# The first feed-forward's input products as seven half-size products for eight, with the gated values in DRAM

## The chip, the cores and the metric

The kernel runs on one core of one Trainium2 chip. The metric is the device time of one execution in microseconds (us); before is the kernel without the change, after the kernel with it. TensorE is called PE here, VectorE DVE, ScalarE ACT, GpSimd POOL and SyncE SP, as the profile names them; PEld is PE's loading of weights.

## The reference, cut to what matters

The whole is a two-layer model with 512 latent and 256 context tokens, and a second block of two layers behind it. The change lies in the feed-forward of the first layer, which runs over all 768 tokens. Its matrices are 1024 x 5632 (`ffn_w_in`, gate and value side by side) and 2816 x 1024 (`ffn_w_out`):

```
def swiglu(h, w_in, w_out):
    a, b = jnp.split(h @ w_in, 2, axis=-1)
    return (jax.nn.silu(a) * b) @ w_out
...
        x = x + g1 * rmsnorm(y_lat, norm_g[l, 1])
        f_lat = swiglu(rmsnorm(x, norm_g[l, 2]) * (1.0 + sc2) + sh2, ffn_w_in[l], ffn_w_out[l])
        x = x + g2 * rmsnorm(f_lat, norm_g[l, 3])
...
            ctx_s = ctx_s + cg1 * rmsnorm(y_ctx, norm_g[l, 1])
            f_ctx = swiglu(rmsnorm(ctx_s, norm_g[l, 2]) * (1.0 + csc2) + csh2, ffn_w_in[l], ffn_w_out[l])
```

`sc2`, `sh2`, `g2` and the like are parts of `silu(c) @ ada_w[l] + ada_b[l]`, for the latent vector `c` and for the context vector. All of it is float32.

## The kernel before

A float32 product is made of three products of a shorter format: each operand is split into a high part `h` (a copy by ACT that rounds) and a low part `l` (a subtraction by DVE), and `mm3` adds `wh*xh`, `wh*xl` and `wl*xh` in PSUM (L329, L330, L331). The splits are `split` for data (ACT L321, DVE L322) and `load_w` for weights (ACT L312, DVE L314). `load_w` loads blocks of 128 x 1024 (512 KB) into `wr`, which has three buffers, by SP's queue (L310); `wh` and `wl` have four each. An instruction waits in its engine's queue, and all that stands behind it there waits too; the order in each queue is set by a scheduler when the kernel is built.

The stretch around the change has three stages.

**Mixer's output.** `layer0_mixer` ends with `out_phase` over `w0_out`. Its last three weight blocks are used tile by tile (six tiles of 128 tokens, 18 matmuls each, `acc`). Behind each tile `residual_norm` takes squares (`sq<-acc`, L337), a product with the gate (`y`, L589) and adds to the residual (`ctx`, `x`, L598). `fill_mod` then normalises the residual for the feed-forward: squares of the row (`sq<-ctx`, `sq<-x`), the reciprocal root on POOL (L342, L343), the scaling `xn` (L355), transposes on PE (`tr`, L363), scale and shift on ACT (`mod`, L375), and the split into `xtf0H` and `xtf0L`.

**Input products** (`ffn_first`, `in_phase`, `in_block`). 44 blocks of `f0_in`, gate and value in turn, so 22 pairs j; each block is multiplied with 256 context and 512 latent tokens, in eight steps k of the model's width, three matmuls each. The first three blocks (the lead) start with the context, which is ready first. A gate's result goes through silu on ACT (L960), a value's is multiplied with it on DVE into `GF` (L962), which lies in SBUF for all 22 blocks. Behind each block two steps of the background are recorded: a step of `ada` loads 512 KB into `wr` (L450) and multiplies it with the rows `srow` (L452, a reduction on DVE for each vector). `ada_rows` loads `srow` (1 MB, L441) and takes silu of it (L443) when this stage begins.

**Output products** (`out_phase` over `f0_out`). Two halves of the output's width, 11 weight blocks each; a block serves two steps k of the hidden width, and each k has six tiles of three matmuls of 512 columns. `Jit` splits `GF[:, k]` just ahead into `jh` and `jl` (two buffers each).

## Time and profile before

| | us |
|---|---|
| median of 3 runs | 3130.43 (3129.79 to 3131.01) |
| the profiled execution, its time | 3131.54 |
| its span in the trace | 3129.8 |
| PE busy | 3055.1, 98% of the span |
| DVE busy | 1903.4, 61% |
| ACT busy | 1294.4, 41% |

The span is what the trace covers, the profiled execution's time 1.7 us more than that. Input products of the first feed-forward lie at about 420 to 792 us of the span, its output products behind them up to about 980 us.

### The profile page before, as it was taken

How to read it: one execution, taken by the hardware profiler on the slowest of the kernel's cores; microseconds unless marked ns; L12 is line 12 of the kernel's file. 1: busy time of each engine (PE TensorE's matmuls, PEld its weight loads, DVE VectorE, ACT ScalarE, POOL GpSimd, SP SyncE). 2: the span in 40 equal slices, each digit the busy share in tenths (PEclk: the TensorE clock that was granted, in tenths of full speed). 3: DMA queues.
4: the chain of work that ended last, by engine and by line, in shares of the span. 5: the costliest groups of instructions: out<-in, count | busy, mean ns of one | idle time of the engine just before them, and what ended most of it. 6: DMA issues, size and time to landing. Idle time of an engine off the chain costs nothing. (4 is left out here: it accounts for less than half of the span.)

```text
span 3129.8 us, 40785 instructions
## 1 busy us (share of the span) xinstructions
PE 3055.1 (98%) x15850; PEld 2567.9 (82%) x15850; DVE 1903.4 (61%) x3252; ACT 1294.4 (41%) x2354; POOL 138.1 (4%) x244
## 2 busy tenths in 40 slices
PE   7999999999998999999999999999999999999999
PEld 6888788888886777888888888788888987788887
DVE  7996677532346677233567777665555687765555
ACT  4333451111335666222455455443334444543334
POOL 1000010000003101000010000000000000000000
PEclk9999999999999999999999999999999999999999
DMA  6621236632221111333322222233333321123332
GB/s 228 186 80 41 95 111 205 204 118 64 74 68 43 55 48 53 103 95 101 95 64 81 68 81 68 81 95 95 97 99 88 104 81 55 54 85 98 95 106 76
DMA packets 80929, 292.31 MB, mean 93 GB/s; under 512 B 9744, under 2 KB 10432, under 8 KB 79840
## 3 DMA queue, kind: packets, MB, share of 16 engines
q1 hardware_dynamic: 79104, 285.48, 30.2%
q0 software_dynamic: 1056, 3.17, 0.3%
q8 instruction: 125, 2.05, 0.3%
q10 hardware_dynamic: 576, 1.05, 0.1%
q14 instruction: 68, 0.56, 0.1%
HBM read 287.54 MB, written 2.12 MB: 93 GB/s over the span
## 5 line engine op out<-in xcount | busy, mean ns | idle before, releaser
L314 DVE TENSOR_TENSOR wl<-wr,wh 128x1024 fp32r<-128x1024 f32 x420 | 513.3, 1224 | 460.2 <-ACT wh L312 456.3
L312 ACT ACTIVATE wh<-wr 128x1024 fp32r<-128x1024 f32 x424 | 447.8, 1057 | 769.6 <-PE in L330 530.4
L329 PE MATMUL acc<-wh,jh 128*128 128x512 f32 x1080 | 424.4, 393 | 7.1 <-ACT jh L321 4.9
L331 PE MATMUL acc<-wh,jl 128*128 128x512 f32 x1080 | 422.0, 393 | 3.4 <-DVE jl L322 3.4
L330 PE MATMUL acc<-wl,jh 128*128 128x512 f32 x1080 | 423.5, 392 | 0.0
L322 DVE TENSOR_TENSOR jl<-GF,jh 128x512 fp32r<-128x512 f32 (+1 forms) x170 | 132.5, 781 | 233.9 <-ACT jh L321 230.2
L329 PEld LDWEIGHTS acc<-wh,jh 128*128 128x128 f32 x1080 | 203.2, 188 | 50.6 <-ACT jh L321 6.6
L321 ACT ACTIVATE jh<-GF 128x512 fp32r<-128x512 f32 (+1 forms) x170 | 119.0, 701 | 300.4 <-PE acc L330 288.8
L330 PE MATMUL in<-xtf0L,wh 128*128 128x256 f32 (+1 forms) x728 | 241.9, 332 | 0.0
L329 PE MATMUL in<-xtf0H,wh 128*128 128x256 f32 (+1 forms) x728 | 241.6, 332 | 0.0
L331 PEld LDWEIGHTS acc<-wh,jl 128*128 128x128 f32 x1080 | 202.9, 188 | 46.8 <-DVE jl L322 5.9
L331 PE MATMUL in<-xtf0H,wl 128*128 128x256 f32 (+1 forms) x728 | 241.2, 331 | 0.0
L330 PEld LDWEIGHTS acc<-wl,jh 128*128 128x128 f32 x1080 | 203.3, 188 | 40.6
L452 DVE SCALAR_TENSOR_TENSOR junkv<-wr,srow 128x1024 bf16<-128x1024 f32 x128 | 156.5, 1222 | 66.3 <-DMA wr<-ada 63.8
L329 PEld LDWEIGHTS in<-xtf0H,wh 128*128 128x128 f32 x728 | 138.3, 190 | 13.6
L331 PEld LDWEIGHTS in<-xtf0H,wl 128*128 128x128 f32 x728 | 138.1, 190 | 13.2
L330 PEld LDWEIGHTS in<-xtf0L,wh 128*128 128x128 f32 x728 | 138.3, 190 | 12.7
L330 PE MATMUL in<-xtf10L,wh 128*128 128x512 f32 (+1 forms) x376 | 141.2, 377 | 0.7 <-DVE xtf10L L322 0.4
L330 PE MATMUL in<-xtv0L,wh 128*128 128x512 f32 (+1 forms) x376 | 141.3, 376 | 0.0
L331 PE MATMUL in<-xtv0H,wl 128*128 128x512 f32 (+1 forms) x376 | 141.3, 376 | 0.0
L331 PE MATMUL in<-xtu0H,wl 128*128 128x512 f32 (+1 forms) x376 | 141.3, 376 | 0.0
L330 PE MATMUL in<-xtu0L,wh 128*128 128x512 f32 (+1 forms) x376 | 141.2, 376 | 0.0
(449 smaller groups left out, 6673.9 us busy)
## 6 DMA issues: line engine op xcount, KB each, us to landing
wr<-f_in SPq DMA_DIRECT2D x88, 512.0 KB, 3.6
wr<-u_in SPq DMA_DIRECT2D x88, 512.0 KB, 3.6
wr<-ada SPq DMA_DIRECT2D x80, 512.0 KB, 4.4
wr<-f_out SPq DMA_DIRECT2D x44, 512.0 KB, 3.6
wr<-u_out SPq DMA_DIRECT2D x44, 512.0 KB, 3.6
wr<-w_in SPq DMA_DIRECT2D x32, 512.0 KB, 3.8
wr<-wm_x SPq DMA_DIRECT2D x32, 512.0 KB, 3.6
wr<-wd_q SPq DMA_DIRECT2D x24, 512.0 KB, 3.5
```

Source lines behind the costliest of these rows:

```text
L312: nc.scalar.activation(h, raw, AF.Copy)
L314: (engine or nc.vector).tensor_sub(l, raw, h.bitcast(FT))
L321: nc.scalar.activation(h, src, AF.Copy)
L322: nc.vector.tensor_sub(l, src, h.bitcast(FT))
L329: mm(out, wh, xh, start=first, stop=False)
L330: mm(out, wh, xl, start=False, stop=False)
L331: self.last_mm = mm(out, wl, xh, start=False, stop=last).ins
L452: nc.vector.scalar_tensor_tensor(self.junkv, raw, 1.0, self.srow[:, v], op0=OP.mult, op1=OP.mult, accum_out=self.mc[l, v][:, j:j + 1])
```

## The change

**Products.** Tokens are cut into two halves of 384 (768 = 2 x 384) and the model's width into two halves of four steps k. A gate block and a value block of weights, each cut at the same width, form a 2 x 2 block matrix, and Strassen's scheme (in Winograd's form) takes seven products of 4 steps and 384 tokens for a pair where the plain way takes eight. `seven_in` makes them: `lead(j)` makes P1 and P2 with the gate block; `finish(j)` makes P6, P5, P7, P3 and P4 with sums of weight blocks (`s12`, `s34`, four additions of 512 columns on DVE) and sums of the data. Of these sums P1 and P2 need none: they use the first 384 tokens as they are (`XA`). Parts of the results are copied out of PSUM in between (`c1`, `u2`, `r5`, `u3`, by ACT) and added on DVE.

**Data.** `ffn_input` replaces `fill_mod`: tokens are normalised into a plain `F`, then split (`XA`, `XB`), then `rest` forms the sums in place (L1026 to L1034) and splits them (`XT`). `rest` is recorded behind the leads of the first two pairs (`LEAD0 = 2`). `ada_rows` moves ahead of `ffn_input`.

**Gated values.** `gf` of a pair is written to DRAM by POOL's queue (384 KB). `Fetch` loads it back in the output products, 384 KB for each k and half, into three buffers `jr` by SP's queue; the six last k of the second half go into `jt`.

**Background.** One step behind each pair in the input products; the others, 40 blocks of `ada` and the gates of layer 1, behind each weight block of the output products, three at a time.

```diff
+class Fetch(Jit):
+    def __call__(self, k):
+        r = self.pool.tile([P, self.T], FT, name="jr", tag="jr", bufs=3)
+        with self.b.tc.high_priority(60):
+            self.b.nc.sync.dma_start(r, self.G[k])
+        h, l = self.pair(self.T)
+        self.b.split(h, l, r)
+        return h, l
+    def tile(self, ks, t):
+        if t == 0:
+            self.last = self.pool.tile([P, len(ks), self.T], FT, name="jt")
+            with self.b.tc.high_priority(200):
+                for i, k in enumerate(ks):
+                    self.b.nc.sync.dma_start(self.last[:, i], self.G[k])
+        h, l = [a.rearrange("p (k t) -> p k t", t=P) for a in self.pair(len(ks) * P)]
+        self.b.split(h, l, self.last[:, :, t * P:(t + 1) * P])
...
+                if after:
+                    after()
...
-        self.prepare(self.pairs("xtf", 1, TOK))
+        self.nes = ExitStack()
+        xp = self.pool("xtf", es=self.nes)
+        half = TOK // 2
+        XA = [xp.tile([P, KT, half], FR, name="xta" + x) for x in "HL"]
+        XB = [xp.tile([P, KT // 2, half], FR, name="xtb" + x) for x in "HL"]
         with ExitStack() as es2:
             op = self.pool("mixo", es=es2)
             jit = Jit(self, jp, MX, TOK, 2)
             rows = [self.gate_row(op, 0, v, 2) for v in range(2)]
             self.out_phase(jit, self.a["w0_out"], KT, range(6),
                            self.residual_norm(op, self.x0, lambda t: rows[1 if t < 2 else 0], 6))
-        self.fill_mod(0, 4, "ng02", ((1, 0, 2), (0, 2, 4)), self.x0, *self.xt[0])
-        self.scres.close()
         es.close()
+        self.adar = ExitStack()
+        self.ada_rows(self.pool("adar", es=self.adar, side="right"))
+        tp = self.pool("xtt", es=self.nes)
+        XT = [tp.tile([P, KT, TOK], FR, name="xtt" + x) for x in "HL"]
+        self.xt = XA, XB, XT
+        self.ffn_input(XA, XB, XT)
...
+        pool = self.pool("scrf", es=es, side="right")
+        new = lambda: pool.tile([P, D], FT, name="xn", tag="xn", bufs=2)
+        spare = [new()]
+        F = pool.tile([P, KT, TOK], FT, name="xtF")
+        H, n = KT // 2, TOK // 2
+        h1, h2 = slice(0, n), slice(n, TOK)
+        def tiles(v, ts):
+            G, B = self.gain(0, v, 4, "ng02"), self.mod(0, v, 3)
+            xn = []
+            for t in ts:
+                ms = pool.tile([P, 1], FT, name="ms", tag="ms", bufs=4)
+                self.squares(pool, self.x0(t), ms)
+                self.rstd(ms, 1)
+                a = spare.pop() if spare else new()
+                nc.vector.tensor_scalar(a, self.x0(t), ms, None, op0=OP.mult)
+                xn.append(a)
+            w = len(ts) * P
+            c = slice(ts[0] * P, ts[0] * P + w)
+            with self.tc.high_priority(100):
+                for k in range(KT):
+                    b = self.bank("tr")
+                    for i, a in enumerate(xn):
+                        nc.tensor.transpose(b[:, i * P:(i + 1) * P], a[:, k * P:(k + 1) * P], self.ident)
+                    nc.scalar.activation(F[:, k, c], b[:, :w], AF.Identity, bias=B[:, k:k + 1], scale=G[:, k:k + 1])
+                    if ts[0] < 3:
+                        self.split(XA[0][:, k, c], XA[1][:, k, c], F[:, k, c])
+                    elif k >= H:
+                        d = slice(c.start - n, c.stop - n)
+                        self.split(XB[0][:, k - H, d], XB[1][:, k - H, d], F[:, k, c])
+        tiles(1, (0, 1))
+        tiles(0, (2,))
+        def rest():
+            tiles(0, (3, 4))
+            tiles(0, (5,))
+            sub = nc.vector.tensor_sub
+            def to_pair(k0, s):
+                for k in range(k0, k0 + H, 2):
+                    self.split(XT[0][:, k:k + 2, s], XT[1][:, k:k + 2, s], F[:, k:k + 2, s])
+            with self.tc.high_priority(100):
+                for k in range(0, H, 2):
+                    a, b = slice(k, k + 2), slice(k + H, k + H + 2)
+                    sub(F[:, a, h1], F[:, a, h2], F[:, a, h1])
+                    sub(F[:, a, h2], F[:, b, h2], F[:, a, h2])
+                    sub(F[:, b, h2], F[:, b, h2], F[:, a, h1])
+                to_pair(H, h2)
+                to_pair(0, h1)
+                to_pair(0, h2)
+                for k in range(0, H, 2):
+                    b = slice(k + H, k + H + 2)
+                    sub(F[:, b, h1], F[:, b, h1], F[:, b, h2])
+                to_pair(H, h1)
+            es.close()
+            self.rest = lambda: None
+        self.rest = rest
...
+        def block(j):
+            r = self.wp.tile([P, KT, P], FT, name="wr", tag="wr", bufs=3)
+            nc.sync.dma_start(r, wap[:, j])
+            return r
+        def pair(src):
+            w = [self.wp.tile([P, KT, P], FR, name="w" + x, tag="w" + x, bufs=4) for x in "hl"]
+            m = src.shape[1]
+            self.split(w[0][:, :m], w[1][:, :m], src)
+            return w
+        h1, h2 = slice(0, n), slice(n, TOK)
+        X = {1: (XA, 0, slice(0, n)), 2: (XA, H, slice(0, n)), 3: (XB, 0, slice(0, n)), 4: (XT, H, h1),
+             5: (XT, 0, h1), 6: (XT, H, h2), 7: (XT, 0, h2)}
+        def product(b, w, w0, q, first, last):
+            wh, wl = w
+            (xh, xl), k0, s = X[q]
+            for i in range(H):
+                self.mm3(b[:, :n], wh[:, w0 + i], wl[:, w0 + i], xh[:, k0 + i, s], xl[:, k0 + i, s],
+                         first and i == 0, i == H - 1, skip_group_check=True)
+        tl = lambda nm, bufs=1: tp.tile([P, n], FT, name=nm, tag=nm, bufs=bufs)
+        def copy(nm, b):
+            t = tl(nm)
+            nc.scalar.activation(t, b[:, :n], AF.Copy)
+            return t
+        def lead(j):
+            with self.tc.high_priority(60):
+                g = block(2 * j)
+                gw = pair(g)
+            x, y = self.bank("in"), self.bank("in")
+            product(x, gw, 0, 1, True, False)
+            product(y, gw, H, 2, True, True)
+            return g, x, y
+        def finish(j, g, x, y):
+            with self.tc.high_priority(90):
+                v = block(2 * j + 1)
+                s12 = tp.tile([P, KT, P], FT, name="s12")
+                s34 = tp.tile([P, KT, P], FT, name="s34")
+                dve.tensor_add(s12[:, :H], v[:, :H], v[:, H:])
+                dve.tensor_sub(s12[:, H:], s12[:, :H], g[:, :H])
+                dve.tensor_sub(s34[:, :H], g[:, :H], v[:, :H])
+                dve.tensor_sub(s34[:, H:], g[:, H:], s12[:, H:])
+                w12, w34, wv = pair(s12), pair(s34), pair(v[:, H:])
+            c1, c2 = copy("c1", x), tl("c2")
+            dve.tensor_add(c1, c1, y[:, :n])
+            nc.scalar.activation(c1, c1, AF.Silu)
+            product(x, w12, H, 6, False, False)
+            u2 = copy("u2", x)
+            z = self.bank("z")
+            product(z, w12, 0, 5, True, False)
+            r5 = copy("r5", z)
+            product(x, w34, 0, 7, False, False)
+            u3 = copy("u3", x)
+            product(z, w34, H, 3, False, True)
+            dve.tensor_add(c2, u2, z[:, :n])
+            nc.scalar.activation(c2, c2, AF.Silu)
+            product(x, wv, 0, 4, False, True)
+            gf = tp.tile([P, TOK], FT, name="gf", tag="gf", bufs=2)
+            dve.tensor_add(u3, u3, r5)
+            dve.tensor_mul(gf[:, n:], u3, c2)
+            dve.tensor_mul(gf[:, :n], x[:, :n], c1)
+            nc.gpsimd.dma_start(GD[j], gf)
+        led = [lead(j) for j in range(LEAD0)]
+        with self.tc.issue_after(self.last_mm):
+            self.rest()
+        tp = self.pool("act0", es=es)
+        for j in range(HID):
+            nxt = led.pop(0) if led else lead(j)
+            finish(j, *nxt)
+            self.run_background(1)
...
-        (XH, XL), = self.xt
         if l == 1:
+            (XH, XL), = self.xt
             self.late.close()
-        gp = self.pool(f"g{l}", es=es, side=("right", "left")[l])
-        GF = gp.tile([P, HID, T], FT, name="GF")
+            gp = self.pool(f"g{l}", es=es, side="left")
+            GF = gp.tile([P, HID, T], FT, name="GF")
+        else:
+            GF = [self.dram.tile([P, T], FT, name=f"gf{j}") for j in range(HID)]
         SL = [(o * P, n * P) for _, o, n in streams]
         st = {}
...
-                self.ada_rows(tp)
-                self.background = chain(self.ada(0, 5, (1, 0)), *[
+                self.background = chain(self.ada(0, 5, (1, 0)), self.all_gates((0, 0, 5), (0, 1, 5)), *[
                     self.ada(1, part, vecs)
                     for part, vecs in ((1, (1, 0)), (0, (1, 0)), (2, (0,)), (4, (0,)), (3, (0,)), (5, (0,)))],
-                    self.all_gates((0, 0, 5), (0, 1, 5), (1, 0, 2), (1, 0, 5)))
-            self.in_phase(XH, XL, self.a[f"f{l}_in"], range(2 * HID), SL, use, 3,
-                          [[(0, 0, 256)], [(1, 0, 256)], [(1, 256, 256)]] if l == 0 else HALVES)
-            self.end_background()
+                    self.all_gates((1, 0, 2), (1, 0, 5)))
+                self.seven_in(es1, self.a["f0_in"], GF)
+            else:
+                self.in_phase(XH, XL, self.a["f1_in"], range(2 * HID), SL, use, 3, HALVES)
+                self.end_background()
...
-            self.out_phase(Jit(self, op, GF, T, 2 if nt > 4 else 3), self.a[f"f{l}_out"], HID, range(nt), res)
+            self.out_phase((Fetch if l == 0 else Jit)(self, op, GF, T, 2 if nt > 4 else 3), self.a[f"f{l}_out"], HID,
+                           range(nt), res, after=lambda: self.run_background(3))
+            if l == 0:
+                self.end_background()
         fill()
+        if l == 0:
+            self.adar.close()
```

In the rows that follow, each line is an instruction in its engine's queue, or so many alike in a run (x4).

On ACT at the end of the mixer's output stood, before (`sq,yms<-acc` are the squares of a finished tile; `sq,ms<-ctx` and `sq,ms<-x` the first work of the feed-forward's input):

```order
L337 ACTIVATE sq,yms<-acc 128x512
L337 ACTIVATE sq,ms<-ctx 128x1024
L337 ACTIVATE sq,yms<-acc 128x512
L321 ACTIVATE jh<-MX 128x768
L337 ACTIVATE sq,ms<-ctx 128x1024
L337 ACTIVATE sq,yms<-acc 128x512
L321 ACTIVATE jh<-MX 128x768
L375 ACTIVATE mod<-tr,mc_80,gain_3448 128x256 x2
L321 ACTIVATE xtf0H<-mod 128x256 x2
```

and now, from the same tile on:

```order
L361 ACTIVATE sq,yms<-acc 128x512
L345 ACTIVATE jh<-MX 128x768
L361 ACTIVATE sq,yms<-acc 128x512 x2
L345 ACTIVATE wh<-wr 128x1024
L467 ACT_TABLE_LOAD
L467 ACTIVATE srow<-srow 128x1024
L361 ACTIVATE sq,yms<-acc 128x512
L467 ACTIVATE srow<-srow 128x1024
L361 ACTIVATE sq,ms<-ctx 128x1024 x2
L361 ACTIVATE sq,ms<-x 128x1024 x2
L1004 ACTIVATE xtF<-tr,mc_80,gain_3467 128x256 x2
L345 ACTIVATE xtaH<-xtF 128x256 x2
```

The work on the feed-forward's input, which stood among the mixer's last tiles, stands behind the last of them and behind the silu of `srow`.

On PE the transposes for the first tokens (`tr`, L363) stood among those tiles, before:

```order
L329 MATMUL acc<-wh,jh 128x512
L363 MATMUL tr<-ident,xn 128x128 x2
L330 MATMUL acc<-wl,jh 128x512
L331 MATMUL acc<-wh,jl 128x512
L329 MATMUL acc<-wh,jh 128x512
L363 MATMUL tr<-ident,xn 128x128 x2
```

and now, at the end of the mixer's tiles (`in<-xta` are P1 and P2),

```order
L355 MATMUL acc<-wh,jl 128x512
L1003 MATMUL tr<-ident,xn 128x128 x20
L353 MATMUL in<-xtaH,wh 128x384
L354 MATMUL in<-xtaL,wh 128x384
L355 MATMUL in<-xtaH,wl 128x384
L1003 MATMUL tr<-ident,xn 128x128
```

and, where the two leads end (`in<-xtt` is P6):

```order
L354 MATMUL in<-xtaL,wh 128x384
L355 MATMUL in<-xtaH,wl 128x384
L1003 MATMUL tr<-ident,xn 128x128 x24
L353 MATMUL in<-xttH,wh 128x384
L354 MATMUL in<-xttL,wh 128x384
```

The transposes of the last 384 tokens stand behind all of the leads' matmuls. On DVE the first weight sums now stand here, behind all work on the data:

```order
L1028 TENSOR_TENSOR xtF<-xtF 128x2x384
L1034 TENSOR_TENSOR xtF<-xtF 128x2x384
L346 TENSOR_TENSOR xttL<-xtF,xttH 128x2x384 x2
L1094 TENSOR_TENSOR s_3788<-wr 128x512
L1096 TENSOR_TENSOR s_3789<-wr 128x512
L1095 TENSOR_TENSOR s_3788<-s_3788,wr 128x512
L1100 TENSOR_TENSOR c_3806<-c_3806,in 128x384
```

(`s_3788` is the first pair's `s12`.) SP's queue held, in the output products before, weight blocks alone (`f_out` x22 in a run). Now it holds, where they begin:

```order
L334 DMA wr<-f_out 128x1024
L474 DMA wr<-ada 128x1024 x3
L334 DMA wr<-f_out 128x1024
L474 DMA wr<-ada 128x1024 x3
L253 DMA jr<-gf_3579 128x768
L253 DMA jr<-gf_3580 128x768
L253 DMA jr<-gf_3581 128x768
L334 DMA wr<-f_out 128x1024
L474 DMA wr<-ada 128x1024
```

and DVE's queue, further on in the first half:

```order
L338 TENSOR_TENSOR wl<-wr,wh 128x1024
L476 SCALAR_TENSOR_TENSOR junkv,mc_81<-wr,srow 128x1024
L346 TENSOR_TENSOR jl<-jr,jh 128x768
L476 SCALAR_TENSOR_TENSOR junkv,mc_81<-wr,srow 128x1024 x2
L346 TENSOR_TENSOR jl<-jr,jh 128x768
L338 TENSOR_TENSOR wl<-wr,wh 128x1024
```

Loads of `ada` stand between the weight blocks and share their three buffers, and their products on DVE stand between the splits.

## Rows read from the trace of the kernel before

**Rows 1.** The page's first part: busy time of PE and share of the span.
```profile
PE 3055.1 (98%) x15850; PEld 2567.9 (82%) x15850; DVE 1903.4 (61%) x3252; ACT 1294.4 (41%) x2354; POOL 138.1 (4%) x244
```

**Rows 2.** Busy time by engine, PEclk, DMA share, GB/s, in two 50 us windows.
```profile
450.00:500.00 50.00, 50.00 (x290) 44.26 (x289) 44.68 (x75) 9.36 (x13) 0.00 (x0) 1.00 0.72 212
...
750.00:800.00 50.00, 48.35 (x269) 42.00 (x268) 13.40 (x15) 10.89 (x14) 1.10 (x2) 1.00 0.28 85
```

**Rows 3.** Timeline of PE, mixer's output: start, duration, instruction; 54 matmuls apart.
```profile
387.83 0.39 PE L329 MATMUL acc<-wh,jh 128*128 128x512 f32 x1
...
400.07 0.39 PE L329 MATMUL acc<-wh,jh 128*128 128x512 f32 x1
```

**Rows 4.** Timeline of ACT in the input products: silu of two neighbouring gates.
```profile
616.99 0.58 ACT L960 ACTIVATE silu<-in 128x512 f32<-128x512 f32 x1
...
633.67 0.58 ACT L960 ACTIVATE silu<-in 128x512 f32<-128x512 f32 x1
```

**Rows 5.** Groups by line and form, 450 to 780 us: busy, mean ns.
```profile
L452 DVE SCALAR_TENSOR_TENSOR junkv<-wr,srow 128x1024 bf16<-128x1024 f32 x74 | 90.6, 1224 | 64.4 <-DMA wr<-ada 63.3
...
L314 DVE TENSOR_TENSOR wl<-wr,wh 128x1024 fp32r<-128x1024 f32 x41 | 50.1, 1223 | 48.0 <-ACT wh L312 47.1
...
L962 DVE TENSOR_TENSOR GF<-in,silu 128x512 f32<-128x512 f32 x20 | 13.8, 688 | 40.9 <-PE in L331 35.8 <-PE rb L484 5.1
```

**Rows 6.** Timeline of ACT from the mixer's output into the input products.
```profile
393.32 0.58 ACT L337 ACTIVATE sq<-acc 128x512 bf16<-128x512 f32 x1
...
396.87 1.06 ACT L337 ACTIVATE sq<-ctx 128x1024 bf16<-128x1024 f32 x1 [2.88 <-DVE ctx L598]
...
405.20 1.02 ACT L375 ACTIVATE mod<-tr,mc,gain 128x256 f32<-128x256 f32 x2 [0.81 <-PE tr L363]
406.11 0.72 ACT L321 ACTIVATE xtf0H<-mod 128x256 fp32r<-128x256 f32 x2
...
420.48 0.57 ACT L337 ACTIVATE sq<-acc 128x512 bf16<-128x512 f32 x1
...
428.31 1.28 ACT L960 ACT_TABLE_LOAD   x1
...
436.30 2.02 ACT L443 ACTIVATE srow<-srow 128x1024 f32<-128x1024 f32 x2
```

**Rows 7.** Timeline of DVE in the same stretch.
```profile
398.97 0.76 DVE L355 TENSOR_SCALAR xn<-ctx,ms 128x1024 f32<-128x1024 f32 x1 [2.13 <-POOL ms L343]
...
406.81 0.76 DVE L322 TENSOR_TENSOR xtf0L<-mod,xtf0H 128x256 fp32r<-128x256 f32 x2
407.48 0.95 DVE L322 TENSOR_TENSOR jl<-MX,jh 128x768 fp32r<-128x768 f32 x1
```

**Rows 8.** Timeline of PE: input products begin in earnest.
```profile
419.53 0.28 PE L330 MATMUL in<-xtf0L,wh 128*128 128x256 f32 x1
```

**Rows 9.** The tile `srow`, 380 to 460 us: its load's time to landing.
```profile
DMA to landing us min/median/max: 7.4/7.4/7.4
```

**Rows 10.** Windows of 1 us around an idle stretch of PE; columns as in Rows 2.
```profile
46.00:47.00 1.00, 0.00 (x0) 0.00 (x0) 1.00 (x3) 0.00 (x0) 1.00 (x1) 1.00 0.49 197
...
48.00:49.00 1.00, 0.22 (x1) 0.22 (x2) 1.00 (x2) 0.00 (x0) 0.45 (x1) 0.50 0.81 315
...
54.00:55.00 1.00, 1.00 (x5) 0.79 (x4) 0.38 (x2) 0.00 (x0) 0.00 (x0) 0.88 0.94 367
```

**Rows 11.** Timeline of ACT where the output products begin.
```profile
791.88 1.06 ACT L312 ACTIVATE wh<-wr 128x1024 fp32r<-128x1024 f32 x1 [6.80 <-PE in L330]
...
797.94 0.85 ACT L321 ACTIVATE jh<-GF 128x768 fp32r<-128x768 f32 x1 [3.54 <-PE acc L330]
802.02 0.85 ACT L321 ACTIVATE jh<-GF 128x768 fp32r<-128x768 f32 x1 [3.23 <-PE acc L330]
```

**Rows 12.** The tile `wr`, 450 to 700 us: time to landing of its 85 loads.
```profile
DMA to landing us min/median/max: 3.4/4.3/6.2
```

**Rows 13.** Windows by DMA: columns as in Rows 2.
```profile
20.00:30.00 10.00, 8.40 (x38) 7.72 (x39) 6.58 (x11) 4.63 (x10) 1.78 (x4) 1.00 0.96 360
450.00:650.00 200.00, 200.00 (x1153) 177.02 (x1152) 131.91 (x211) 36.43 (x50) 0.00 (x0) 1.00 0.67 205
```

More of the change, by code (lines that the diff above doesn't have):

```diff
@@ L28 @@
 EPS = 1e-6
+LEAD0 = 2
 LINE = 128
@@ L242, in tile @@
         return t.rearrange(f"p ({' '.join(names)}) -> p {' '.join(names)}", **dict(zip(names, shape[1:])))
+class Fetch(Jit):
[14 more added lines that the diff above has]
+        self.b.split(h, l, self.last[:, :, t * P:(t + 1) * P])
+        return h, l
 class Body:
@@ L325, in split, with mm3 @@
             nc.vector.scalar_tensor_tensor(l, src, scale, h.bitcast(FT), op0=OP.mult, op1=OP.subtract)
-    def mm3(self, out, wh, wl, xh, xl, first, last):
+    def mm3(self, out, wh, wl, xh, xl, first, last, **kw):
         mm = self.nc.tensor.matmul
-        mm(out, wh, xh, start=first, stop=False)
-        mm(out, wh, xl, start=False, stop=False)
-        self.last_mm = mm(out, wl, xh, start=False, stop=last).ins
+        mm(out, wh, xh, start=first, stop=False, **kw)
+        mm(out, wh, xl, start=False, stop=False, **kw)
+        self.last_mm = mm(out, wl, xh, start=False, stop=last, **kw).ins
     def squares(self, pool, x, total):
@@ L539, in in_block, with out_phase @@
                 use(j, i, b[:, :a + n])
-    def out_phase(self, pair, wap, nk, tiles, use, tail=3, order=None, first=0):
+    def out_phase(self, pair, wap, nk, tiles, use, tail=3, order=None, first=0, after=None):
         for hf in range(2):
@@ L937, in pool_group, with ffn_input @@
             nc.scalar.activation(MX[:, g, o:o + L], b[:, :L], AF.Copy, scale=self.p("pool_scale", g))
+    def ffn_input(self, XA, XB, XT):
+        nc = self.nc
+        es = ExitStack()
+        pool = self.pool("scrf", es=es, side="right")
[52 more added lines that the diff above has]
+        self.rest = rest
@@ new lines, in seven_in @@
+    def seven_in(self, es, wap, GD):
+        nc = self.nc
+        XA, XB, XT = self.xt
+        H, n = KT // 2, TOK // 2
+        dve = nc.vector
+        def block(j):
[66 more added lines that the diff above has]
+            self.run_background(1)
@@ L953, in ffn_first @@
         with ExitStack() as es1:
-            tp = self.pool(f"act{l}", es=es1)
+            if l == 1:
+                tp = self.pool("act1", es=es1)
             def use(j, i, b):
```

## The prediction

> **What bounds the kernel now.** The page's first part comes first: PE is busy for 98% of the span [rows 1], so a matmul taken away counts unless PE then waits for something. The windows say where that holds: at 450 to 500 us, in the input products, PE is busy for 50.00 of 50 us at full clock, while DVE has 5 us left and ACT 41 [rows 2]; where the output products follow it loses 1.65 of 50. So the change's stage is bound by matmuls alone, and a saving of them is real in its middle. What it does at its two ends and in the stage behind is the question.
>
> Two timelines give the prices. In the mixer's output 54 matmuls of 512 columns lie between 387.83 and 400.07, so one takes 0.2267 us [rows 3]. One pair takes 633.67 - 616.99 = 16.68 us [rows 4]; it holds 48 matmuls of 512 columns and 48 of 256, so one of 256 takes 16.68/48 - 0.2267 = 0.1208.
>
> **1. Products: -45.9 us.** For 384 columns, which the trace does not show, I take the mean of the two, 0.1737 (the bounds are the two themselves; the size lies midway). A pair is now 7 x 4 x 3 = 84 matmuls, 14.60 us; 22 pairs take 321.1 instead of 367.0. The cover is DVE and ACT. On DVE a pair has 3.5 weight subtractions at 1.22, four sums of 512 columns at 0.69 at most, five operations of 384 columns at some 0.55 and one `ada` step with two vectors, 2 x 1.31 [rows 5]: 12.4 of 14.6 us. ACT has less. On PE's queue P3 waits for the copy `r5`, behind a weight copy on ACT, while P7's 12 matmuls (2.1 us) run; walked with these durations 0.4 us are left there and about 1 us at the wait of P6 for `c1`. I take nothing for these waits; if 0.3 us a pair were lost it would be +6.6.
>
> **2. The start: +36.7 us against the products' saving.** Before, input work stands among the mixer's last tiles; that stretches those tiles (the last one's squares start at 420.48 instead of 393.32 + 5 x 18 x 0.2267 = 413.7), but PE is in the input products from 419.53 on [rows 6, 8], and by 466 us it has done some 46 us of them. After, by the order, it goes so:
> - The mixer's matmuls end at 413.7. The load of `srow` takes the place in SBUF of the mixer's splits, so it is issued behind the last `jl`, at about 406.6; it lands in 7.4 us [rows 9], at 414.0. ACT then has a table load (1.28), two silu (1.01 each) and the squares of the last tile, all ahead of the first `sq<-ctx`, which starts at 418.0; two squares of 1.06 later begin those of `x`, and the scaled row of the second tile is ready 2.1 + 0.76 us behind its squares' start (396.87 to 398.97) [rows 6, 7], at 421.9. Before, the first of these squares began at 396.87.
> - Eight pieces of 256 columns and eight of 128 take scale, shift and rounding on ACT: 0.51 + 0.36 a step k for 256, some 0.3 + 0.27 for 128, together 11.6 us [rows 6]: 422.3 to 433.9. The leads (48 matmuls, 8.34 us) follow them step by step from about 429.5.
> - PE has then been idle for 16 us. Where it idled before 48.8 us the granted clock was 0.50 at 48 to 49 us and came back only at 54 to 55 [rows 10]. The leads therefore end at some 440.6.
> - The transposes of the last 384 tokens stand behind them. The third `xn` needs one of two buffers that the first transposes free, so it comes at 445.0; the sums of the data begin at 446.5. Eight sums and eight low parts of 768 columns at 0.95 on DVE, with the small pieces between, take 17 us [rows 7]: 463.5. `s12` stands behind all of them: 1.9, and the rounding of it 1.06. P6 of the first pair starts at 466, with bounds of 462 (ACT and DVE overlap better) and 470.
> - Then 321.1 - 8.3 = 312.8 us of products are left, 2.7 for the clock's second warm-up and 1.5 for the first small waits: they end at 783.0. Before, their last weight was freed at 791.88 and the output products ran from about 793 [rows 11]. Of 45.9 us, 9.2 are left: 36.7 are eaten by the start.
>
> **3. The join: +3.5.** Before, `GF` is at hand, and 1.7 us pass. After, the first `gf` can be fetched only when the buffers of the input products are free: by SP's order behind two weight blocks and six `ada` loads, the last of which waits for a weight subtraction in the last pair. Walked, it is issued 0.8 us before the last matmul of P4, lands 4.5 later and is split in 0.85 + 0.95 behind two `ada` products on DVE: 5.2 us. Bounds 2 and 8 (the latter with a clock that falls).
>
> **4. The output products: +7.6, and +2 at the change of halves.** Two steps k take 2 x 4.08 = 8.16 us on PE [rows 11]. In this time SP's queue now brings one weight block, three `ada` blocks of 524 KB and two `jr` of 393 KB, 2.88 MB, 353 GB/s; before it was one block. DVE has 3 x 1.31 + 1.22 + 2 x 0.95 = 7.1 us, which fits. The limit is the three buffers of `wr`. A load is issued when the block three before it is used up, lands after L, and is used up after 1.3 (`ada`) or 2.3 us (rounding and subtraction). Followed round three buffers, three weight blocks' turns take 4 L + 7 us (four loads, the four uses in between and the issues). That is 24.5 us, PE's own pace, for L = 4.4. In the input products of before the 85 loads landed in 3.4 to 6.2, median 4.3 [rows 12], at 205 GB/s with the DMA engines 67% busy [rows 13]. At 1.7 times the rate L will not be less. I take 4.9, nearer to the median than to the maximum, since the number of loads in flight on `wr` stays three: (4 x 4.9 + 7)/3 = 8.87, so 0.71 a turn. The first eight `ada` blocks, with two vectors, are mostly used up before the join; the 32 others fill 10.7 turns: 7.6 us. Bounds: L = 4.3 gives 0, L = 6.2 gives 26. At the change of halves six evictions of 0.69 (as for 512 columns in [rows 5]) stand ahead of the splits on DVE: 2.
>
> The same from the side of the rate: 205 GB/s at 0.67 would be 306 GB/s with the engines full, which is 9.4 us a turn and +13; 360 GB/s, which 20 to 30 us show at 0.96 [rows 13], would be 8.0 and +0. The value taken lies between. The Trainium skill ("DMA: Bandwidth & Descriptors", Specifications) gives about 358 GB/s as one core's share of HBM; by it the 353 wanted here would just fit and this term would be 0. The windows of this trace do not settle it: they reach that rate, but not in loads of this kind.
>
> From the layer-1 mixer on the queues are the same. One microsecond is added for the tail of the stage.
>
> **Sum.** -9.2 + 3.5 + 7.6 + 2 + 1 = +4.9. Terms are taken from one execution of 3131.54, 1.1 above the median of 3130.43; as a difference it holds for both: 3130.4 + 4.9, about 3135.
>
> **The rivals.** Faster or slower means by more than 0.2% (6.3 us), about what this kernel's measurement can tell from nothing.
> - *The forecast*: the start eats most and the output products give a little back: L of 4.4 to 5.3, 3128 to 3141 by the sum. Chance 0.42.
> - *More of the saving survives the start.* Every microsecond that P6 starts ahead of 466 is one gained; from 455 on the change is faster, 3124, and at 443, where the leads have just ended and the sums of the data would run beside them, 3112. For it: each delay is one queue's order, and such waits were covered before. Against: the order on ACT, PE and DVE has no way past them. Chance 0.25.
> - *The output products are bound by loads.* Place: the three `wr` buffers with `ada` between the weights; price: 1.33 us a turn for each us of L; it decides from L = 5.0 on (9.0 a turn, 9.0 us over 10.7 turns for the sum's 7.6, which makes 6.3 in all), and gives 3142 at 5.4 and 3154 at 6.2. For it: 306 GB/s from [rows 13]. Against: the rate of 360. Chance 0.23, for L above 5.3.
> - *The pairs are not bound by PE*: the waits for `r5` and `c1` cost 0.3 to 0.6 us a pair, +7 to +13: 3142 to 3148. For it: 0.4 us of slack in a walk. Against: DVE at 12.4 of 14.6. Chance 0.10.
>
> **How the numbers follow.** The time is the forecast's, 3135. The second case is faster, 0.25. The last two are slower, 0.33, and of the forecast's 0.42 I put 0.12 above 3136.7, where slower begins (L from 5.0 to 5.3, or P6 at 468 to 470); the other 0.30 are within 0.2%. So 0.25, 0.30, 0.45. The range leaves out 1 in 10 at each side: 3114, in the lower part of the second case, and 3152, where L nears the trace's maximum. The forecast's own is 3128 to 3141.
>
> **What would show it.** Right: silu of neighbouring pairs 14.6 us apart; `sq<-ctx` at 418, PE idle from 413.7 to about 429 and again until P6 at 466 with a granted clock of 0.50 behind each; the first `jh` of the output products some 5 us behind the last product; `jh` there 8.9 us apart for two k while `ada` runs, and 8.16 behind it; landing of `wr` at 4.9 in the median. Wrong: P6 before 460 or behind 472; pairs of over 15 us; turns of 8.2 (loads fit) or over 9.5; a price for 384 columns that is not the mean of its neighbours.

## The result and the profile after

After takes 3153.62 us (median of 4 runs, 3151.75 to 3157.86), before 3130.72 beside it: a ratio of 1.0074, 95% interval 1.0061 to 1.0086. The change makes the kernel slower by 0.7%. The page's first part, to be read against [rows 1]: PE is busy for 25 us less, and the span is 21.8 us longer.

```profile
span 3151.6 us, 40674 instructions
PE 3030.0 (96%) x15514; PEld 2567.2 (81%) x15514; DVE 2036.9 (65%) x3466; ACT 1382.3 (44%) x2502; POOL 148.8 (5%) x266
```

The busy time falls by less than the 45.9 us of the products, since it also counts matmuls that run at the lower clock (the granted clock is 0.989 in the mean, 0.997 before); how the rest splits was not worked out. That the products themselves were saved is seen in the pairs below, and more than the saving is lost in waits. First and last matmuls of the stages, from the timeline of PE in both traces (us):

| | before | after | difference | forecast |
|---|---|---|---|---|
| P6 of the first pair starts | | 461.8 | | 466 |
| input products end | 792.07 | 792.65 | +0.6 | -9.2 |
| from there to the first matmul of the output products (the join) | 1.65 | 8.44 | +6.8 | +3.5 |
| output products, first to last matmul | 185.9 | 200.0 | +14.1 | +9.6, and 1 for the tail |
| span | 3129.8 | 3151.6 | +21.8 | +4.9 |

Nearly all of the difference, 21.5 us, has arisen by the end of the output products (979.6 before, 1001.1 after). Windows of after, columns as in [rows 2] (busy time of PE, PEld, DVE, ACT, POOL, then PEclk, DMA share, GB/s), show where PE stands:

```profile
400.00:450.00 50.00, 34.27 (x148) 25.03 (x146) 28.45 (x49) 38.02 (x87) 10.34 (x24) 0.79 0.06 22
450.00:500.00 50.00, 38.19 (x205) 37.25 (x206) 47.49 (x71) 23.57 (x35) 1.18 (x2) 0.84 0.41 122
600.00:650.00 50.00, 50.00 (x291) 49.91 (x290) 33.33 (x47) 22.80 (x37) 1.62 (x3) 1.00 0.28 89
750.00:800.00 50.00, 40.38 (x228) 39.42 (x228) 37.02 (x62) 17.55 (x28) 2.94 (x6) 0.98 0.55 175
800.00:810.00 10.00, 8.91 (x33) 7.25 (x34) 8.21 (x13) 3.59 (x4) 0.00 (x0) 0.78 1.01 382
850.00:900.00 50.00, 47.24 (x203) 37.05 (x201) 36.26 (x54) 17.47 (x27) 0.00 (x0) 1.00 0.88 304
```

PE has full work at 600 to 650 and in no other of these. What it waited for from 400 to 1010 us (total, times, longest), in the view of waits:

```profile
PE in L353 <- ACT wh L345: 16.7, 1, 16.7
PE in L353 <- ACT c L1077: 11.0, 9, 2.1
PE acc L353 <- ACT jh L345: 8.4, 1, 8.4
PE tr L1003 <- DVE xn L995: 7.1, 3, 5.5
PE acc L355 <- DVE jl L346: 6.0, 10, 1.9
```

The first and the fourth are the start, the second the pairs, the third the join, the last the output products. The second was put at nothing in the forecast.

**The start.** PE waits for the rounding of the first `s12`. DVE has no gap of more than 0.2 us from 442.55 until the sums for it are made. Timeline of DVE, then of PE:

```profile
442.55 1.98 DVE L1026 TENSOR_TENSOR xtF<-xtF 128x768 f32<-128x768 f32 x2 [0.65 <-ACT xtF L1004]
...
456.91 1.95 DVE L346 TENSOR_TENSOR xttL<-xtF,xttH 128x768 fp32r<-128x768 f32 x2
458.78 0.69 DVE L1094 TENSOR_TENSOR s<-wr 128x512 f32<-128x512 f32 x1
```
```profile
461.81 0.69 PE L353 MATMUL in<-xttH,wh 128*128 128x384 f32 x1 [16.72 <-ACT wh L345]
```

From here to 466 us matmuls start 0.32 us apart instead of 0.17: PE has been idle, the granted clock is 0.50 from 450 to 460 (1.2 GHz) and 0.68 in the mean of 460 to 470.

All of this lies some 4 us earlier than forecast. `srow` was loaded sooner and faster, so that ACT took its table load with no wait for it (timeline of SP, landing of `srow`, timeline of ACT):

```profile
405.20 0.33 SPq L465 DMA_DIRECT2D srow<-c  x1
```
```profile
DMA to landing us min/median/max: 4.7/4.7/4.7
```
```profile
410.08 1.28 ACT L467 ACT_TABLE_LOAD   x1
```

**The pairs.** The silu of c1 (L1101), once a pair, on ACT's timeline, without `ada` blocks and with them:

```profile
610.43 0.50 ACT L1101 ACTIVATE c<-c 128x384 f32<-128x384 f32 x1
625.00 0.50 ACT L1101 ACTIVATE c<-c 128x384 f32<-128x384 f32 x1
...
670.24 0.52 ACT L1101 ACTIVATE c<-c 128x384 f32<-128x384 f32 x1
686.20 0.53 ACT L1101 ACTIVATE c<-c 128x384 f32<-128x384 f32 x1
```

14.57 us against 15.96. The six pairs between 566 and 655 us, beside which DVE has no `ada` product, take 14.55 to 14.69; the eight behind them, with `ada`, 15.55 to 16.97. In one of the slower pairs SP, DVE, ACT and PE show this (four timelines):

```profile
532.48 0.33 SPq L474 DMA_DIRECT2D wr<-ada  x1
538.65 1.47 SPq L1053 DMA_DIRECT2D wr<-f_in  x2
```
```profile
538.54 1.22 DVE L476 SCALAR_TENSOR_TENSOR junkv<-wr,srow 128x1024 bf16<-128x1024 f32 x1
...
544.57 0.69 DVE L1094 TENSOR_TENSOR s<-wr 128x512 f32<-128x512 f32 x1 [3.20 <-DMA wr<-f_in]
545.18 0.55 DVE L1110 TENSOR_TENSOR c<-u,z 128x384 f32<-128x384 f32 x1
```
```profile
545.82 0.53 ACT L1111 ACTIVATE c<-c 128x384 f32<-128x384 f32 x1 [2.67 <-DVE c L1110]
...
549.12 0.49 ACT L1077 ACTIVATE c<-in 128x384 f32<-128x384 f32 x1 [2.25 <-DVE gf L1116]
```
```profile
549.66 0.44 PE L353 MATMUL in<-xttH,wh 128*128 128x384 f32 x1 [1.25 <-ACT c L1077]
```

A pair needs three loads into the three `wr` buffers: gate, value and `ada`. The second `ada` product ends at 539.7; the next value block's load (the second of the `x2`) is issued right then, and DVE can use it 4.8 us later. DVE stands 3.2 us at the first sum of this block, which PE needs only a pair later; but behind it in DVE's queue stand L1110 and the products `gf` of the present pair. ACT's silu of c2 and the next copy c1 wait for these, and PE for the copy.

**The join and the output products.** The last input product ends at 792.65. The first `jr` is issued 2.1 us later, behind three `ada` loads in SP's queue, the last of which got its buffer of `wr` when a weight subtraction on DVE ended; the first `jh` follows its landing (timelines of DVE, SP and ACT):

```profile
793.07 1.22 DVE L338 TENSOR_TENSOR wl<-wr,wh 128x1024 fp32r<-128x1024 f32 x1
```
```profile
788.48 6.17 SPq L474 DMA_DIRECT2D wr<-ada  x3
794.74 1.33 SPq L253 DMA_DIRECT2D jr<-gf  x3
```
```profile
800.20 0.84 ACT L345 ACTIVATE jh<-jr 128x768 fp32r<-128x768 f32 x1 [4.83 <-DMA jr<-gf]
```

PE's clock is 0.78 in the mean of 800 to 810. Time to landing from 800 to 920 us, first of `wr`, then of `jr` (780 to 1000):

```profile
DMA to landing us min/median/max: 3.7/5.4/7.0
```
```profile
DMA to landing us min/median/max: 3.0/4.7/7.1
```

That of `wr` was 4.3 in [rows 12]. The `jh` of odd k, for k = 3 and k = 21, and further on a weight block of the second half (timelines of ACT, SP and ACT):

```profile
810.84 0.85 ACT L345 ACTIVATE jh<-jr 128x768 fp32r<-128x768 f32 x1 [3.23 <-PE acc L354]
...
890.06 0.85 ACT L345 ACTIVATE jh<-jr 128x768 fp32r<-128x768 f32 x1 [3.06 <-PE acc L354]
```
```profile
911.55 0.33 SPq L334 DMA_DIRECT2D wr<-f_out  x1
```
```profile
918.40 1.06 ACT L336 ACTIVATE wh<-wr 128x1024 fp32r<-128x1024 f32 x1 [4.97 <-DMA wr<-f_out]
```

Two k take (890.06 - 810.84)/9 = 8.80 us, where before has 8.16. Set beside the same `jh` of before, the 14.1 us of the stage arise so: 1.4 up to k = 3 (the lower clock), 5.8 in the nine turns to k = 21, 2.1 at the change of halves, and 4.6 at the weight block above, which is issued at 911.55 and rounded at 918.40; PE waits 2.5 us for it, and the clock is 0.83 from 920 to 930.

### The profile page after: what moved, and what is told of

It reads as the page before. It is cut to its first block, busy times and chain, and to the rows that moved or that the text cites. A ratio compares the mean times of both kernels' runs of the same rounds, so it can differ in the third digit from the quotient of the medians.

```text
span 3151.6 us, 40674 instructions
## 1 busy us (share of the span) xinstructions
PE 3030.0 (96%) x15514; PEld 2567.2 (81%) x15514; DVE 2036.9 (65%) x3466; ACT 1382.3 (44%) x2502; POOL 148.8 (5%) x266
## 5 line engine op out<-in xcount | busy, mean ns | idle before, releaser
L338 DVE TENSOR_TENSOR wl<-wr,wh 128x1024 fp32r<-128x1024 f32 x376 | 459.2, 1223 | 415.9 <-ACT wh L336 412.6
L336 ACT ACTIVATE wh<-wr 128x1024 fp32r<-128x1024 f32 x380 | 401.2, 1057 | 565.2 <-PE in L354 392.3
L346 DVE TENSOR_TENSOR jl<-GF,jh 128x512 fp32r<-128x512 f32 (+1 forms) x126 | 90.2, 718 | 139.7 <-ACT jh L345 137.9
L345 ACT ACTIVATE jh<-GF 128x512 fp32r<-128x512 f32 (+1 forms) x126 | 81.9, 652 | 196.2 <-PE acc L354 184.6
L355 PE MATMUL in<-xtf10H,wl 128*128 128x512 f32 (+1 forms) x376 | 141.0, 376 | 0.0
L353 PE MATMUL in<-xtv0H,wh 128*128 128x512 f32 (+1 forms) x376 | 140.9, 376 | 0.0
L353 PE MATMUL in<-xtu0H,wh 128*128 128x512 f32 (+1 forms) x376 | 140.8, 376 | 0.0
L353 PE MATMUL in<-xtf10H,wh 128*128 128x512 f32 (+1 forms) x376 | 140.7, 376 | 0.0
L1412 DVE SCALAR_TENSOR_TENSOR cv<-in,prm,cv 128x511 f32<-128x511 f32 (+1 forms) x176 | 131.3, 746 | 3.0
L353 PE MATMUL in<-xttH,wh 128*128 128x384 f32 x264 | 90.8, 344 | 27.9 <-ACT wh L345 16.7
```

Of the source, the lines that this page charges most:

```text
L336: nc.scalar.activation(h, raw, AF.Copy)
L338: (engine or nc.vector).tensor_sub(l, raw, h.bitcast(FT))
L345: nc.scalar.activation(h, src, AF.Copy)
L346: nc.vector.tensor_sub(l, src, h.bitcast(FT))
L353: mm(out, wh, xh, start=first, stop=False, **kw)
L355: self.last_mm = mm(out, wl, xh, start=False, stop=last, **kw).ins
```

## The experiments

All times in this section are medians, spans of stages are from one trace of each run. The kernel before, measured beside them, took 3130.49 (e1 to e4), 3128.92 (e5 to e8) and 3129.01 (e9 to e12). A stage also moves where the edit leaves it alone: in such traces P6 starts at 459.9 to 461.8, the input products take 326.1 to 331.7 us from there, and the output products 196.5 to 203.2. Differences inside these bounds are not read as effects.

**e1: own buffers for `ada` in the input products.**

```diff
-            raw = self.wp.tile([P, D], FT, name="wr", tag="wr", bufs=3)
+            if self.ap:
+                raw = self.ap.tile([P, D], FT, name="wa", tag="wa", bufs=3)
+            else:
+                raw = self.wp.tile([P, D], FT, name="wr", tag="wr", bufs=3)
...
+        self.ap = self.pool("adaw", es=self.adar, side="right")
         tp = self.pool("act0", es=es)
...
                 self.seven_in(es1, self.a["f0_in"], GF)
+                self.ap = None
```

> The ada blocks of the input products go into three buffers of their own; in the output products they use wr as in the changed kernel. Theory (three wr buffers are the limit: the next value block is issued only when an ada product has freed a buffer, and the sums s12 wait for it): the pairs with an ada block take 14.6 us like those without, not 16.0, the input products end 12 to 15 us earlier, 3139 to 3142 us. Rival (DVE's load or the rate of loads is the limit): those pairs stay at 15.5 to 16, 3150 to 3154.

3138.54 us, 15 us less than after. Windows of PE (columns as above), with `ada` in the first and without in the second:

```profile
500.00:550.00 50.00, 50.00 (x291) 50.00 (x290) 49.72 (x82) 22.53 (x34) 2.16 (x4) 1.00 0.62 190
...
700.00:750.00 50.00, 50.00 (x290) 50.00 (x289) 33.07 (x48) 22.08 (x34) 2.16 (x4) 1.00 0.30 94
```

DVE is busy for 49.72 of 50 us and PE has no gap, although nine `ada` blocks are loaded from 498 to 560 us where after loads four. From P6 to the end the input products take 317.6 us instead of 330.8. The buffers were the limit, not DVE's load nor the rate. The join is shorter too, 5.0 us: the first `jr` is issued 0.4 us ahead of the last product's end.

**e2: own buffers for `ada` in the output products alone.** The same edit, with the buffers in the output products' pool.

```diff
+            self.ap = op if l == 0 else None
             res = self.residual_norm(op, x_of, lambda t: rows[vec[t]], nt)
```

> The ada blocks of the output products go into three buffers of their own; in the input products they use wr as in the changed kernel. Theory (the three wr buffers and the landing time behind one another): two steps k take 8.16 us nearly throughout although the same bytes are loaded, the join is shorter by 2 to 4 us since gf is no longer queued behind six ada loads, 3135 to 3140 us. Rival (the rate of 350 GB/s is the limit): landing over 5 us and two steps k still at 8.8 or more, 3148 to 3154.

3152.79 us: nearly nothing. The theory fails here. Two k take 8.16 us from 810 to 872, on weight blocks loaded beforehand, and then the lost time comes back: DVE stands at an `ada` block with the splits behind it.

```profile
891.23 1.23 DVE L480 SCALAR_TENSOR_TENSOR junkv<-wa,srow 128x1024 bf16<-128x1024 f32 x1 [5.50 <-DMA wa<-ada]
892.38 0.08 DVE L480 DVE_READ_ACCUMULATOR junkv<-wa,srow 128x1 f32 x1
892.38 0.95 DVE L347 TENSOR_TENSOR jl<-jr,jh 128x768 fp32r<-128x768 f32 x1
```

From 820 to 850 the core loads 320 to 342 GB/s with the DMA engines at 0.95; the rival's sign, the rate, is there, though not its 8.8 for two k throughout. The join became longer, 14.1 us in place of 8.4. The stage takes 198.1 us.

**e3: three blocks of `gf` fetched once.** `Fetch` keeps three tiles and reads `self.kept[k % 3]`.

> Only three blocks of gf are fetched and used again and again in the output products (other numbers, and the last six k of the second half still fetched); all else as in the changed kernel. Theory (landing time of wr sets the turn, and the 0.79 MB of gf a turn lengthen it): landing of wr falls from 5.4 to about 4.4, two steps k take about 8.2, 3140 to 3145 us. Rival (the fetch costs nothing, the ada blocks alone fill the buffers): landing stays over 5, 3151 to 3154. Rival (what costs is that gf itself comes late): only the join changes, by under 3 us.

3151.21 us. The landing of `wr` falls to 4.3, as the theory has it, but the stage takes 198.8 us, within the bounds above: two k take 8.42 in the mean (8.16 to 9.5) while `ada` runs. Neither taking bytes away nor giving buffers alone shortens the stage clearly.

**e4: `rest` recorded ahead of the leads.**

```diff
+        self.rest()
         led = [lead(j) for j in range(LEAD0)]
-        with self.tc.issue_after(self.last_mm):
-            self.rest()
```

> The work on the last 384 tokens (rest) is recorded ahead of the two leads instead of behind them. Theory (at the start a chain of transposes, sums and splits stands behind the leads, and PE waits 16.7 us for it): P6 starts 7 to 10 us earlier, about 453, the leads lie inside the wait, 3143 to 3147 us. Rival (ACT and DVE are the limit, whatever PE's order): P6 still at 460 or later, 3151 to 3155.

3149.60 us; P6 starts at 460.2, where it also starts in runs without this edit, although transposes of the last tokens now stand among the leads. The rival holds: order on PE is not what sets P6.

**e5: in the output products `ada` blocks not loaded.** One tile, loaded once, serves all `ada` products there.

> In the output products the ada products on DVE all read one block that is loaded once (other numbers); their loads are left out there, gf is fetched as in the changed kernel. Theory (loads, not DVE's products, hold the output products up: 2.9 MB a turn of two k at some 305 GB/s): two k take 8.16 us throughout, the stage from first jh to its end is 10 to 13 us shorter, 3139 to 3144 us. Rival (the ada products standing between the splits in DVE's queue hold them up): turns stay at 8.5 or more, 3148 to 3154.

3142.71 us. PE has no gap from 800 to 900, with DVE 47 to 48 us busy of 50 (columns as above); the stage takes 188.5 us, of which the clock behind the join (0.96 in the first window) takes 2. The join is longer, 12.1 us.

```profile
800.00:850.00 50.00, 50.00 (x212) 40.94 (x212) 47.99 (x74) 14.68 (x17) 0.00 (x0) 0.96 0.61 196
850.00:900.00 50.00, 50.00 (x222) 41.38 (x222) 47.21 (x73) 19.81 (x31) 0.00 (x0) 1.00 0.52 164
```

The loads hold the stage up, not the products on DVE.

**e6: e2 and e3 at once.**

> Both at once in the output products: ada in three buffers of their own, and only three blocks of gf fetched and used again (other numbers). Theory (two limits, each enough alone: the rate with gf and ada together, the three wr buffers without gf): two k take 8.16 us, 3140 to 3146 us, though either edit alone gave 1 to 2 us. Rival (something else, DVE's order or the join, keeps the stage long): turns stay at 8.5 or the join takes 14 us, 3149 to 3153.

3144.98 us, and 193.6 for the stage, where e2 has 198.1 and e3 198.8. Against the 200.0 of after the two edits together give 6.4 us; the 1.9 and 1.2 of each alone lie within the bounds above. The join takes 12.4 us, and 193.6 is still 7.7 more than before.

**e7 and e8: all of the computation, with the limits avoided.** `ada` has its own buffers throughout, and more of it runs in the input products.

```diff
             finish(j, *nxt)
-            self.run_background(1)
+            self.run_background(2)
...
-                           range(nt), res, after=lambda: self.run_background(3))
+                           range(nt), res, after=lambda: self.run_background(1))
```

e8 has besides that the edit of e4, two buffers for `ada`, and `jr` in a pool that is free before the input products end:

```diff
-        r = self.pool.tile([P, self.T], FT, name="jr", tag="jr", bufs=3)
+        r = self.b.jrp.tile([P, self.T], FT, name="jr", tag="jr", bufs=3)
```

> All of the computation; ada in three buffers of its own, two background steps behind each pair of the input products (38 ada blocks there) and one behind each weight block of the output products (18 there). Theory: pairs at 14.6 us (DVE at about 13.4 a pair), turns at 8.16 with 1.8 MB each, so the input products end near 777 and the rest is before's plus the join's 5: 3118 to 3124 us, faster than before. Rival (DVE becomes the limit of the pairs, or ada's loads hold the join up as in e2): pairs at 15 or a join of 14, 3128 to 3136.

> As e7, with rest ahead of the leads, the buffers jr outside the space that the input products hold, so that the first three blocks of gf are fetched early, and two buffers for ada instead of three. Theory (the join waits for the fetch alone): the join falls from 5 to 14 us to about 2, 4 to 8 us less than e7: 3111 to 3118 us. Rival (the join waits for weights or DVE, or two buffers are too few): as e7 or slower, 3118 to 3126.

e7: 3133.81 us, the rival's size: input products end at 776.1, but the join takes 13.2 us. e8: 3124.11 us (ratio to before 0.9984, 0.9975 to 0.9993), 10 us less than e7 and faster than both kernels. The time lies in the rival's range, but the join does what the theory says: it takes 1.8 us, as before. Its waits:

```profile
PE in L354 <- ACT wh L346: 16.9, 1, 16.9
PE acc L356 <- DVE jl L347: 7.5, 7, 1.4
PE tr L1007 <- DVE xn L999: 6.5, 3, 5.5
...
PE acc L354 <- ACT jh L346: 1.6, 1, 1.6
```

What is left is the start, and 7.5 us in the output products, which take 193.2 us; their `ada` blocks run there (304 GB/s from 780 to 850).

**e9: two buffers for c1.** `t = tl(nm, 2 if nm == "c1" else 1)` in `copy`.

> The tile c1 has two buffers instead of one; ada stays in the three wr buffers. Theory (in a pair with an ada block DVE stands 3 us at the sum of a value block whose load got its buffer late; PE waits only because behind it stands the product that frees c1, and the next pair's copy needs c1): the pairs with ada fall from 16.0 to 14.6 to 15.0 us without any other buffers, 3139 to 3146 us. Rival (the sums themselves come too late for PE): P6 waits for the rounded sum instead, pairs stay at 16, 3151 to 3155.

3148.87 us; pairs with `ada` still take 15 to 17 us, and the input products 329.2 from P6 on, within the bounds above. What the median gains lies in the output products (196.5), which the edit does not touch. In the pair around 545 the copy c1 no longer waits for `gf`, but ACT stands 5.07 us at the silu of c2 ahead of it, for the same L1110 on DVE behind the same late block.

```profile
545.82 0.52 ACT L1111 ACTIVATE c<-c 128x384 f32<-128x384 f32 x1 [5.07 <-DVE c L1110]
```

The one buffer was not the link; the wait has moved to the next instruction that stands behind the late block in DVE's and ACT's queues.

**e10: the kernel before with gated values through DRAM, and nothing else of the change.**

> The kernel before with one part of the change alone: gated values go to DRAM and are fetched back, products and background as before. Theory (the fetch alone fits beside the weight blocks, 1.3 MB a turn; it costs the join, where the first fetch waits for the space of the input products): turns 8.16, join 5 to 12 us longer, 3135 to 3143 us. Rival (the fetch costs nothing, the join of the changed kernel is due to the ada loads ahead of it): 3129 to 3133.

3141.52 us, 12.5 more than before, as the theory had it. The join takes 12.0 us; two k take 8.16.

```profile
PE acc L351 <- ACT jh L343: 12.0, 1, 12.0
```

The first `jr` is issued 2.6 us behind the last input product, behind a weight block's load that had waited for a weight subtraction. Three `jr`, one `jt` and two gate rows (`grow`, 512 KB each) are issued within 3.1 us there; the longest `jr` takes 9.5 us to land and `grow` 6.9 and 8.7. The clock is 0.50 from 796 to 806. All five runs with a join of 12 to 14 us (e2, e5, e6, e7, e10) issue both gate rows within 1 us ahead of the first `jr`; the six with 5 to 11 (after, e1, e3, e4, e9, e11) issue one, 2.9 us behind it. No run moves the gate rows alone, so this is not shown to be the cause.

**e11: the eight sums of the data left out** (`sub = lambda *a: None`).

> The eight sums of the data at the start are left out (other numbers): splits and products use the plain data. Theory (from the last transposes on DVE's queue, sums and low parts, sets P6): P6 starts 6 to 8 us earlier, at about 454, 3145 to 3148 us. Rival (ACT's roundings or the weights' load set it): P6 at 459 or later, 3151 to 3154.

3145.20 us; P6 starts at 453.1, 6.8 to 8.7 us earlier than where the start is unchanged, about the time of eight sums at 0.95. DVE's queue sets the end of the start.

**e12: e8 with these sums on POOL** (`sub = nc.gpsimd.tensor_sub`).

> As e8, with the eight sums of the data on POOL instead of DVE. Theory (DVE's queue sets P6, and POOL can make the sums beside DVE's low parts): P6 2 to 6 us earlier than in e8, 3119 to 3122 us. Rival (POOL takes so long for a sum, or slows DVE so, that the chain through the sums is longer): P6 later, 3125 to 3135.

3130.24 us, the rival. A sum takes 1.80 to 2.40 us on POOL (0.95 on DVE), and the low parts on DVE beside them 1.96 in the median instead of 0.95. P6 starts 5 us later than in e8, at 464.1.

## Why the prediction was wrong

The direction was seen as likeliest by a little, the size was not: 22.9 us slower where 4.9 were forecast, just outside of the range. Against the forecast P6 came 4.2 us earlier, which hid a part of the loss; the input products took 13.8 us longer from there, the join 3.2 and the output products 4.5.

- **Step 1, the price of the products: right.** 14.57 us a pair is 0.1734 for a matmul of 384 columns; the mean of the neighbours was 0.1737.
- **Step 1, the cover: the step that failed.** "I take nothing for these waits" holds for `r5` and for `c1` as they were walked, and for pairs without `ada`. But DVE's 12.4 of 14.6 us was a sum of busy time and asked nothing of when its operands land. The ring of three `wr` buffers was followed in step 4 for the output products and not here, where it also carries three loads a pair. The input products took 13 us longer from P6 on than in e1, where 317.6 us meet the forecast's 317. The fourth rival (pairs not bound by PE) gave the right size, 7 to 13, and one of its places, the wait of P6 for `c1` (11.0 us in the view of waits). Its reason, 0.4 us of slack in a walk, was another: only pairs with `ada` lose, the later eight 1.0 to 2.4 us each, to a load behind which DVE's and ACT's queues stand. It came together with the others, and each rival was priced alone.
- **Step 2, the start: right in kind, 4.2 us too long.** 466 was forecast, 461.8 measured. The load of `srow` was issued at 405.20 for the forecast's 406.6 and landed in 4.7 us, not in the 7.4 of [rows 9]; with no wait for it `sq<-ctx` began at 413.86 for the forecast's 418. From the first sum of the data to P6 it took what was forecast, 19.3 us for 19.5, and e11 shows DVE's queue to be the limit.
- **Step 3, the join: mis-sized.** 8.4 us where 5.2 were taken, just above the upper bound of 8. The queue was read rightly: the first `jr` stands behind the `ada` loads, the last of which waits for a weight subtraction. But it was issued 2.1 us behind the last product's end and not 0.8 ahead of the last matmul, and took 5.4 us to land, not 4.5. The join is long without `ada` loads too: e10 has 12.0, by the same two terms (issued 2.6 us behind the end, landing in up to 9.5). e1, where `jr` is issued ahead of the end, has 5.0, and e8, where the first blocks of `gf` are fetched early, has none of it.
- **Step 4, the output products: nearly the right term for a reason that is only half right.** 8.80 us for two k against 8.87, in all +14.1 against 9.6 and 1; the change of halves took the 2 that were forecast. One late weight block (4.6) and the clock behind the join (1.4) were not in the sum. The landing time was 5.4, not 4.9, and by the formula this would be 9.5 us, so that 8.80 came out near is in part luck. e2, e3 and e6 fit a reading in which the formula's ring is one of two limits: free of the ring, the stage is held by the rate; free of part of the bytes, by the ring; clearly shorter it is only with both eased (e6) or the loads gone (e5). The Trainium skill ("DMA: Bandwidth & Descriptors", Specifications) gives about 358 GB/s for a core's share of HBM, by which the loads wanted would fit. The traces reach and pass this figure in single stretches of 10 us (359 GB/s from 835 to 845 in e2, 382 from 800 to 810 in after), but do not hold it: after loads 311 GB/s from 800 to 900 with the DMA engines at 0.90, and e2 314 from 820 to 890 at 0.92.

Open is what share the rate and the ring each have in the 14 us; e5 shows only that the loads together hold the stage up, and the two limits are argued from e2, e3 and e6. The median of e4 is 4 us below that of after while P6 lies where it does without the edit; this was not followed up.

## What to carry to other kernels

Busy time of a covering engine is not cover: where a queue runs in order, ask for each of its operands when its load gets a buffer, and who stands behind it. When background loads share a ring with the loads of a faster loop, count loads per turn against buffers in both stages, the old and the new. A value that moved from SBUF to DRAM cost most at the first fetch here (the join of e10 is 10.4 us longer than before's): give that a space which is free early.

## What the runs showed of the hardware that was not expected

A subtraction of 128 x 768 takes DVE 0.95 us, but 1.96 in the median and up to 2.38 while POOL makes such subtractions beside it; POOL's take 1.80 to 2.40 (e12, view of the tiles `xttL` and `xtF`, the durations in ns):

```profile
L347 DVE TENSOR_TENSOR xttL<-xtF,xttH x8: 946/1960/2380, 441.6 to 460.2; 128x768 fp32r<-128x768 f32 x8
```
```profile
L1038 POOL TENSOR_TENSOR xtF<-xtF x2: 2395/2396/2396, 448.4 to 456.8; 128x768 f32<-128x768 f32 x2
```

So two engines together were slower than DVE alone: P6 came 5 us later than in e8.
